# Four DRAM tensors of a hybrid layer kernel in another layout: transposed keys and queries by chunk, neighbourhood values by pair of heads and column block

## The chip, the cores and the metric

The kernel runs on one core of a Trainium2 chip. Five engines work side by side, each through its own instructions in order: TensorE (PE in the profile; PEld is its weight load), VectorE (DVE), ScalarE (ACT), GpSimd (POOL) and SyncE (SP). SP does no arithmetic here; it issues the kernel's DMAs, which run on 16 DMA engines. The metric is the device time of one execution in microseconds, lower is better; a version's time is the median of several runs.

## The reference

One layer over 1024 latent tokens (a grid of 16 rows by 64 columns) and 256 context tokens, width 1024. After a modulated RMS norm and one input projection the columns are split between two groups.

```python
dn_c, s_ctx_f, s_ctx_b = gated_deltanet(pc[..., :DN_IN], ..., s_zero, s_zero)
dn_x, _, _ = gated_deltanet(px[..., :DN_IN], ..., s_ctx_f, s_ctx_b)
qx, kx, vx = na_qkv(px[..., DN_IN:], na_q_norm_w[i], na_k_norm_w[i])
qc, kc, vc = na_qkv(pc[..., DN_IN:], na_q_norm_w[i], na_k_norm_w[i])
na_x = neighborhood_attention(qx, kx, vx, kc, vc, na_rpb[i], rows)
x = x + g1 * (jnp.concatenate([dn_x, na_x], axis=-1) @ w_out[i])
x = x + g2 * swiglu(modulate(rms_norm(x, norm2_w[i]), sh2, sc2), w_ffn_in[i], w_ffn_out[i])
```

Group A (`gated_deltanet`, 4 heads of 128) passes q, k and v through a short convolution and scans them in chunks, forward and backward, context first. In a chunk the state S meets the keys and the queries:

```python
v_new = u_i - jnp.einsum("bhck,bhkv->bhcv", w_i, S)
o_i = (jnp.einsum("bhck,bhkv->bhcv", q_i * jnp.exp(gam_i)[..., None], S)
       + jnp.einsum("bhcm,bhmv->bhcv", qk_i, v_new))
```

Group B (`neighborhood_attention`, 8 heads of 64): each query attends to a window of 8 rows by 16 columns of the grid and to all context keys. The grid's columns are cut into 4 blocks of 16 queries, and a block's keys lie in 32 columns.

## The kernel before

Work runs in stages: modulation and norm; the blocks of the input projection; the scans with the attention beside them; the output projection; the feed-forward part, which takes nearly half of the time. Between the first stages and the scans, intermediate results go through DRAM tensors (names that end in `_d`). The change touches four:

- `kT_d` (128, 4, T): the transposed keys of group A, channel of a head, head, token. `Block.norm` of a "k" block writes one head (L540): 128 pieces of 5 KB.
- `qT_d` (128, 4, L): the same for queries (L544).
- `nv_d` (T, 512): the neighbourhood's values by token. `Wide.tiles` writes it: ten products of 128 tokens, evacuated by ACT into `zt` (L665), stored two at a time (L669), each half of the columns in a `Wide` job of its own.
- `vw_d` (128, 4, 4, 512): partition (four grid rows by 32 columns), column block, row block, the values of all heads. The generator `windows` (L1089) copies it together from `nv_d`, DRAM to DRAM: sixteen copies, one for each column block `cb` and row block `ch`, of 128 pieces of 2 KB (L1093).

The columns of the projection are worked through as `jobs` (L1076): "k" blocks, `Wide(1)`, "nk" blocks, `Wide(0)`, "nk" 3, "nq" blocks, "q" blocks, "v", "z". In the loop at L1109 a job's matmuls are followed by evacuation (`evac`: L491), the square for the norm (L532), `norm` (L549 to L574) and `finish` of the blocks before it. The weights of the next job are fetched by `prefetch`: SP loads 512 KB into `wraw`, of which there is one buffer (L219), ACT casts them into `whi`, of which there are two (L220), GpSimd makes the remainder `wlo` (L222).

Beside the jobs run background generators: `block_inverses` (DVE's eliminations L947 and L949, transposes on PE, results to `x_d` at L969 and L972), then `preps` (fetches L997 to L1003, decays L1015, products L1024). `copies` runs `windows` with two steps behind each k of a job (L1164), from the job after `Wide(0)` on.

Readers of the tensors: a "q" block's `finish` loads its head's keys again as `kTh` (L594). In the scans, `load` (L270) fetches a chunk's `kT` (L280) and `qT` (L289), four heads by 128 tokens: 512 pieces of 512 B each. In the attention, `values` (L329) fetches `vw` for a pair of heads and a column block (L332): again 512 pieces of 512 B. Each of these loads is 256 KB. The loads of `v`, `y`, `kt`, `at` and `kk`, of the same size, have 128 pieces of 2 KB.

The order of instructions on an engine is set by a planner that arranges what the program writes by the times it expects; only where the code asks for it (`pinned`, `held`) is the written order kept. An engine then takes its instructions strictly in that order, and SP its DMAs.

Of the kernel before, what the change touches and what calls it, by code (L numbers as in the profile page):

```python
# [9 lines left out]
F32 = mybir.dt.float32  # L10
# [9 lines left out]
D, L, CT, T = 1024, 1024, 256, 1280  # L20
# [6 lines left out]
NCH = T // 128  # L27
NU = NCH * NH
BLKS = [0, 8, 24, 32]
# [62 lines left out]
def hybrid(ctx, tc, a, dbg):  # L92
    nc = tc.nc
    act, dve, pool, sp = nc.scalar, nc.vector, nc.gpsimd, nc.sync
# [16 lines left out]
    def pools(stack, name, side=None, bufs=1, **kw):  # L111
        if side:
            kw["side"] = side
        return stack.enter_context(tc.tile_pool(name=name, bufs=bufs, reuse_waits="tile", **kw))
# [6 lines left out]
    dram = ctx.enter_context(tc.tile_pool(name="dram", bufs=1, space=DRAM))  # L121
# [37 lines left out]
    v_d = dram.tile([T, 512], F32, name="v_d", tag="v_d")  # L159
    k_d = dram.tile([T, 512], F32, name="k_d", tag="k_d")  # L160
    zT_d = dram.tile([128, 4, L], F32, name="zT_d", tag="zT_d")
    kT_d = dram.tile([128, 4, T], F32, name="kT_d", tag="kT_d")
    qT_d = dram.tile([128, 4, L], F32, name="qT_d", tag="qT_d")
    kk_d = dram.tile([128, NCH, 4, 128], F32, name="kk_d", tag="kk_d")
    qk_d = dram.tile([128, 8, 4, 128], F32, name="qk_d", tag="qk_d")
    nv_d = dram.tile([T, 512], F32, name="nv_d", tag="nv_d")
    nq_d = dram.tile([NAH, 2, ND, L], F16, name="nq_d", tag="nq_d")
    nk_d = dram.tile([2, NAH, ND, T], F16, name="nk_d", tag="nk_d")
    vw_d = dram.tile([128, 4, 4, 512], F32, name="vw_d", tag="vw_d")
    y_d = dram.tile([2, NCH, 128, 4, 128], F32, name="y_d", tag="y_d")  # L170
    at_d = dram.tile([2, 8, 128, 4, 128], F32, name="at_d", tag="at_d")
    x_d = dram.tile([128, 2, 2, NU, 32], F32, name="x_d", tag="x_d")
# [97 lines left out]
    def load(d, c, own=None):  # L270

        def tile(n):
            if own:
                return own.tile([128, 4, 128], F32, name=n, tag=f"{n}{d}")
            return (scan_v if n == "v" else scan_in).tile([128, 4, 128], F32, name=n, tag=n, bufs=3)

        old = chunks.pop(c, None)
        kT, qT, kt, v = old or (tile("kT"), tile("qT") if c >= 2 else None, tile("kt"), tile("v"))
        if not old:
            sp.dma_start(kT, kT_d[:, :, c * 128:(c + 1) * 128])  # L280
            sp.dma_start(fl(v), v_d[c * 128:(c + 1) * 128])
        y = tile("y")
        sp.dma_start(y, y_d[d, c])
        if not old:
            sp.dma_start(fl(kt), k_d[c * 128:(c + 1) * 128])
        at = None
        if c >= 2:
            if not old:
                sp.dma_start(qT, qT_d[:, :, (c - 2) * 128:(c - 1) * 128])  # L289
            at = tile("at")  # L290
            sp.dma_start(at, at_d[d, c - 2])
        if not old and c in TWICE:
            chunks[c] = kT, qT, kt, v
        ready[d, c] = kT, qT, kt, v, y, at
# [5 lines left out]
    def attention(nw):  # L300
# [18 lines left out]
        def biases(hp, half, cb):  # L319

            key = hp, half, CASE[cb]
            if tables[0] != key:
                out = lasting_bt[tables[1] % 2]
                for u, w0 in enumerate(WIN):
                    sp.dma_start(out[u][:, w0:w0 + 384], a["rpb"][2 * hp + u, half, CASE[cb]])
                tables[:] = key, tables[1] + 1
            return lasting_bt[(tables[1] - 1) % 2]

        def values(hp, half, cb):  # L329
            if (hp, cb) not in blocks:  # L330
                vw = nw.tile([128, 4, 128], F32, name="vw", tag="vw", bufs=3)
                sp.dma_start(vw, vw_d[:, cb, :, hp * 128:hp * 128 + 128])  # L332
                blocks[hp, cb] = vw
            return blocks[hp, cb][:, half:half + 3]

# [57 lines left out]

        order = [(hp, half, cb) for hp in range(NAH // 2) for cb, half in TILES]
        heads = {0: [load(0), load(1)]}
        vcs = {0: context(0)}
        bt, vw = biases(*order[0]), values(*order[0])
        yield 1
        old = None
        for n, (hp, half, cb) in enumerate(order):  # L400
            at = n % len(TILES)
            if at in (4, 6) and hp + 1 < NAH // 2:
                heads.setdefault(hp + 1, []).append(load(2 * hp + at // 2))
                if at == 4:
                    vcs[hp + 1] = context(hp + 1)
            cur = pair(heads[hp], bt, vw, vcs[hp], half, cb, na[hp])
            next(cur)
            if old:
                next(old)
            if n + 1 < len(order):  # L410
                bt, vw = biases(*order[n + 1]), values(*order[n + 1])
            yield 1
            if old:
                next(old)
            old = cur
            yield 1
# [5 lines left out]
    with ExitStack() as bs:  # L422
        wp = pools(bs, "wpb", "right", 2)
        shift(bs, "hpad", "right", 64)
        hp = pools(bs, "hp", "right")
# [4 lines left out]
        def bank(name="m"):  # L430

            if len(psum) == 1:
                return psum[0].tile([128, 512], F32, name=name, tag="ps")
            return psum[1].tile([128, 512], F32, name=name, tag=name, bufs=4 if name == "blk" else 2)
# [19 lines left out]
        class Block:  # L454
# [79 lines left out]
            def norm(self):  # L534

                kind, acc, t0, i = self.kind, self.acc, self.t0, self.i
                if kind in "vz":
                    return
                if kind == "k":
                    sp.dma_start(kT_d[:, i], acc)  # L540
                    return
                r = self.r
                if kind == "q":
                    sp.dma_start(qT_d[:, i], acc[:, t0:])  # L544
                    return
                for s0, n in self.segs:
                    p = bank("pr" if kind == "nk" and s0 >= 768 else "m")
                    pe.matmul(p[:, :n], M[C_BD2], r[:, s0:s0 + n], start=True, stop=True)
                    act.activation(r[:, s0:s0 + n], p[:, :n], AF.Ln, bias=b_eps, scale=1.0 / ND)  # L549
                if kind == "nq":  # L550
                    act.activation(r[:, t0:], r[:, t0:], AF.Exp, scale=-0.5, bias=b_naq)
                else:
                    act.activation(r[:, t0:], r[:, t0:], AF.Exp, scale=-0.5)
                isk = kind == "nk"
                u = acc
                dve.scalar_tensor_tensor(u[:, t0:], u[:, t0:], qkw[:, isk:isk + 1], r[:, t0:],
                                         op0=OP.mult, op1=OP.mult)
                hl16 = cp.tile([128, 2, T], F16, name="hl16", tag="kx", bufs=3)
                h16, l16 = hl16[:, 0], hl16[:, 1]
                if isk:  # L560
                    act.copy(h16, u)
                    dve.tensor_tensor(l16, u, h16, OP.subtract)
                else:
                    for hf in range(2):
                        s = slice(t0 + hf * 512, t0 + hf * 512 + 512)
                        uv = u[:, s].rearrange("p (r b c) -> p b r c", r=8, b=4)
                        hv, lv = (x[:, s].rearrange("p (b r c) -> p b r c", b=4, r=8) for x in (h16, l16))
                        act.copy(hv, uv)
                        dve.tensor_tensor(lv, uv, hv, OP.subtract)
                for i, x in enumerate((h16, l16)):  # L570
                    for hb in range(2):
                        hd = 2 * self.i + hb
                        dst = nk_d[i, hd] if isk else nq_d[hd, i]
                        sp.dma_start(dst, x[hb * 64:hb * 64 + 64, t0:])  # L574

            def finish(self):
                kind, acc, i = self.kind, self.acc, self.i
                if kind in "kv":
                    vt = cp.tile([128, NCH, 128], F32, name="vt", tag="kx", bufs=3)
                    for g, m in ((0, 4), (4, 4), (8, 2)):  # L580
                        p = bank()
# [9 lines left out]
                    sp.dma_start(dst[:, i * 128:(i + 1) * 128].rearrange("(c p) d -> p c d", p=128), vt)  # L591
                if kind == "q":
                    kT = cp.tile([128, T], F32, name="kTh", tag="kx", bufs=3)
                    sp.dma_start(kT, kT_d[:, i])  # L594
                    p, r, t0 = bank(), self.r, self.t0
                    for c in range(8):
                        pe.matmul(p[:, c:c + 1], r[:, t0 + c * 128:t0 + (c + 1) * 128], M[C_ONE][:, 0:1],
                                  start=True, stop=True)
                    dve.tensor_copy(SQ[:, :, i], p[:, 0:8])
                    yield  # L600
                else:
                    kT = acc
                if kind in "kq":
                    c0 = 0 if kind == "k" else 2
                    kk = cp.tile([128, NCH, 128], F32, name="kk", tag="kx", bufs=3)
                    for g in range(c0, NCH, 4):
                        m = min(4, NCH - g)
                        p = bank()
# [480 lines left out]
        def windows():  # L1089
            vlat = nv_d[CT:].rearrange("(r c) d -> r c d", c=64)  # L1090
            for cb in range(4):
                for ch in range(4):
                    sp.dma_start(vw_d[:, cb, ch], vlat[4 * ch:4 * ch + 4, BLKS[cb]:BLKS[cb] + 32])  # L1093
                    yield

        copies = Background()
# [12 lines left out]
        for n in range(2, len(jobs) + 2):  # L1109
# [59 lines left out]
            if isinstance(j, Wide) and n == values:  # L1169
                copies.add(windows())  # L1170
# [202 lines left out]
    acc = nrm.tile([128, L], F32, name="acc", tag="acc")  # L1373
# [488 lines left out]
```

## Time and profile before

| | |
|---|---|
| median of three runs | 1512.64 us (1511.35 to 1515.03) |
| the profiled execution | 1511.45 us |
| its span, first to last instruction | 1509.7 us |
| mean granted TensorE clock | 0.99 |
| DMA moved | 267.35 MB in 198851 packets, of which 106960 under 2 KB |

Stages, from the chain in order of time: projection blocks to about 552 us, scans and attention from there to about 770 us, output projection to about 860 us, feed-forward to the end. The page gives, part by part, each engine's busy time, the span in 40 slices, the DMA queues, and the chain of work that ended last. Views of the trace give the same for chosen stretches: a timeline lists instructions in order of time (start, duration, engine and line, operation, out<-in by name, count), the waits name who waited for whom (us in total, times, longest), and the view of a tensor gives the durations of its instructions (least, median, most in ns). "SPq" is SP issuing a DMA: its duration is that of the issue, not of the transfer. In the chain, "DMA a<-b" is the time from the issue to the landing.

### The profile page before, as it was taken

The page shows a single profiled execution, that of the slowest core. Times are in us where ns is not written, and L with a number is a line of the kernel's source. Part 1 is how long each engine was busy: PE and PEld are TensorE (multiplying, and loading weights), DVE is VectorE, ACT ScalarE, POOL GpSimd, SP SyncE. Part 2 cuts the span into 40 slices and gives each one's busy share as a digit, 9 for nine tenths or more (in the row PEclk, how much of TensorE's full clock was granted, in tenths as well). Part 3 has the DMA queues.
Part 4 walks back from the last instruction along what each step waited for, and adds up shares of the span by engine and source line. Part 5 has one row for each costly group of instructions (what it writes and reads, how often), then busy time and mean ns, then how long its engine had stood idle before and what let it go on. Part 6 is the DMA issues. An engine that isn't in the chain of part 4 may idle for free.

```text
span 1509.7 us, 23086 instructions
## 1 busy us (share of the span) xinstructions
PE 1453.5 (96%) x8365; PEld 1205.7 (80%) x8365; DVE 1007.9 (67%) x1908; ACT 704.7 (47%) x1379; POOL 164.6 (11%) x191
## 2 busy tenths in 40 slices
PE   6999998799999999999989999999999999999998
PEld 2789887678877778898777888788888888888887
DVE  4886579445587418789966499655555666698652
ACT  6443362585256536667732374333333334354441
POOL 0153500243134300000000000000000000000000
PEclk9999999999999999999999999999999999999999
DMA  9377133566378799986339216333333325798742
GB/s 366 119 237 234 35 107 121 180 180 194 98 235 249 214 272 289 264 225 184 116 119 313 99 35 208 106 105 105 105 105 105 104 94 173 267 365 281 237 153 84
DMA packets 198851, 267.35 MB, mean 177 GB/s; under 512 B 15232, under 2 KB 106960, under 8 KB 197712
## 3 DMA queue, kind: packets, MB, share of 16 engines
q1 hardware_dynamic: 198016, 265.49, 55.1%
q8 instruction: 66, 1.08, 0.3%
q10 hardware_dynamic: 720, 0.37, 0.1%
q14 instruction: 49, 0.40, 0.1%
HBM read 201.01 MB, written 68.98 MB: 179 GB/s over the span
## 4 chain that ended last, share of the span: by engine, by line
PE 67%; DVE 8%; DMA 5%; ACT 5%; issue 2%; SPq 1%; POOL 0%; ACTq 0%; DVEq 0%; POOLq 0%
PE ps L102 45%; PE blk L102 10%; PE sc L102 5%; PE pr L102 3%; DMA nv_d<-zt 2%; PE sc L106 2%; PE m L102 1%; DMA wad<-wa 1%; DMA wraw<-w_nqk 1%; DVE acc L256 1%; ACT ex L366 1%; DVE x L1616 1%; DVE cacc L520 1%; SPq L1093 1%; DVE ex L368 0%
## 5 line engine op out<-in xcount | busy, mean ns | idle before, releaser
L102 PE MATMUL ps<-hT,uhi 128*128 128x512 f32 x496 | 146.8, 390 | 0.9 <-DVE e L1737 0.8
L102 PE MATMUL ps<-lT,uhi 128*128 128x512 f32 x496 | 146.4, 389 | 0.0
L102 PE MATMUL ps<-hT,ulo 128*128 128x512 f32 x496 | 146.2, 389 | 0.0
L102 PE MATMUL blk<-hh,whi 128*128 128x512 f32 (+1 forms) x456 | 139.3, 397 | 2.1 <-ACT hh L748 1.8
L102 PE MATMUL blk<-hl,whi 128*128 128x512 f32 (+1 forms) x456 | 130.1, 379 | 0.0
L102 PE MATMUL blk<-hh,wlo 128*128 128x512 f32 (+1 forms) x456 | 129.9, 378 | 0.0
L102 PE MATMUL ps<-hB,uhi 128*128 128x512 f32 x436 | 129.1, 390 | 0.0
L102 PE MATMUL ps<-lB,uhi 128*128 128x512 f32 x436 | 128.9, 389 | 0.0
L102 PE MATMUL ps<-hB,ulo 128*128 128x512 f32 x436 | 128.7, 389 | 0.0
L1446 ACT CAST uhi<-ws 128x512 fp32r<-128x512 f32 x91 | 54.7, 623 | 145.4 <-PE ps L102 75.8
L1446 ACT CAST uhi<-wq 128x512 fp32r<-128x512 f32 x101 | 60.4, 621 | 130.8 <-PE ps L102 66.3
L1447 DVE TENSOR_TENSOR ulo<-wq,uhi 128x512 fp32r<-128x512 f32 x101 | 67.1, 686 | 65.6 <-ACT uhi L1446 36.1
L102 PEld LDWEIGHTS ps<-hT,uhi 128*128 128x128 f32 x496 | 92.9, 188 | 20.7 <-ACT uhi L1446 1.2
L102 PEld LDWEIGHTS ps<-lT,uhi 128*128 128x128 f32 x496 | 93.0, 188 | 19.7 <-DVE lT L1600 0.4
L102 PEld LDWEIGHTS ps<-hT,ulo 128*128 128x128 f32 x496 | 93.1, 188 | 19.4
L102 PEld LDWEIGHTS ps<-hB,uhi 128*128 128x128 f32 x436 | 81.8, 188 | 17.4 <-issue 0.5
L102 PEld LDWEIGHTS ps<-lB,uhi 128*128 128x128 f32 x436 | 81.8, 188 | 17.3 <-DVE lB L1600 0.4
L102 PEld LDWEIGHTS ps<-hB,ulo 128*128 128x128 f32 x436 | 81.8, 188 | 17.0
L102 PEld LDWEIGHTS blk<-hh,wlo 128*128 128x128 f32 x456 | 80.9, 191 | 17.9 <-issue 1.7
L102 PEld LDWEIGHTS blk<-hl,whi 128*128 128x128 f32 x456 | 81.6, 192 | 15.5
L102 PEld LDWEIGHTS blk<-hh,whi 128*128 128x128 f32 x456 | 77.3, 192 | 19.4 <-ACT hh L748 3.7
L1447 DVE TENSOR_TENSOR ulo<-ws,uhi 128x512 fp32r<-128x512 f32 x91 | 60.6, 685 | 36.2 <-ACT uhi L1446 28.1
(337 smaller groups left out, 3020.1 us busy)
## 6 DMA issues: line engine op xcount, KB each, us to landing
wq<-w_fo SPq DMA_DIRECT2D x99, 256.0 KB
wq<-w_gu SPq DMA_DIRECT2D x88, 256.0 KB
wad<-wa SPq DMA_DIRECT2D x64, 256.0 KB
t_d<-g SPq DMA_DIRECT2D x22, 512.0 KB
fr<-t_d SPq DMA_DIRECT2D x44, 256.0 KB
bt<-rpb SPq DMA_DIRECT2D x48, 192.0 KB
f_d<-g SPq DMA_DIRECT2D x33, 256.0 KB
fr<-f_d SPq DMA_DIRECT2D x33, 256.0 KB
```

The costliest lines, as they stand in the source:

```text
L102: i = nc.tensor.matmul(*args, **kw)
L106: i = nc.tensor.transpose(*args, **kw)
L256: dve.scalar_tensor_tensor(acc2, x, sc, acc2, op0=OP.mult, op1=OP.add)
L366: act.activation(ex, ex, AF.Exp, bias=m[:, 1:2], accum_out=m[:, 2:3])
L520: dve.scalar_tensor_tensor(acc[:, d0:d1], raw[:, d0 + o:d1 + o], cw[:, blk, tap:tap + 1], acc[:, d0:d1], op0=OP.mult, op1=OP.add)
L1093: sp.dma_start(vw_d[:, cb, ch], vlat[4 * ch:4 * ch + 4, BLKS[cb]:BLKS[cb] + 32])
L1446: act.copy(hi, self.raw[key])
L1447: dve.tensor_tensor(lo, self.raw[key], hi.bitcast(F32), OP.subtract)
L1616: dve.tensor_tensor(B[at][:, k], B[x][:, k], B.get(y, B["B11"])[:, k], OP.subtract)
```

## The change

The four tensors are declared, written and read in another order of dimensions. `kT_d` and `qT_d` get the chunk ahead of the head; `vw_d` gets the pair of heads ahead of the column block, and its last dimension is 128, one pair. A load in the scans or the attention then takes 128 pieces of 2 KB. The stores of `kT_d` and `qT_d` and the reload `kTh` go by chunk, in pieces of 512 B. `windows` copies one grid row at a time, 32 columns by four pairs of heads: 64 copies of 128 pieces of 512 B, four ahead of each `yield` where there was one. No arithmetic changes.

```diff
-    kT_d = dram.tile([128, 4, T], F32, name="kT_d", tag="kT_d")
-    qT_d = dram.tile([128, 4, L], F32, name="qT_d", tag="qT_d")
+    kT_d = dram.tile([128, NCH, 4, 128], F32, name="kT_d", tag="kT_d")
+    qT_d = dram.tile([128, 8, 4, 128], F32, name="qT_d", tag="qT_d")
...
-    vw_d = dram.tile([128, 4, 4, 512], F32, name="vw_d", tag="vw_d")
+    vw_d = dram.tile([128, 4, 4, 4, 128], F32, name="vw_d", tag="vw_d")
...
-            sp.dma_start(kT, kT_d[:, :, c * 128:(c + 1) * 128])
+            sp.dma_start(kT, kT_d[:, c])
...
-                sp.dma_start(qT, qT_d[:, :, (c - 2) * 128:(c - 1) * 128])
+                sp.dma_start(qT, qT_d[:, c - 2])
...
-                sp.dma_start(vw, vw_d[:, cb, :, hp * 128:hp * 128 + 128])
+                sp.dma_start(vw, vw_d[:, hp, cb])
...
-                    sp.dma_start(kT_d[:, i], acc)
+                    sp.dma_start(kT_d[:, :, i], acc.rearrange("p (c t) -> p c t", t=128))
...
-                    sp.dma_start(qT_d[:, i], acc[:, t0:])
+                    sp.dma_start(qT_d[:, :, i], acc[:, t0:].rearrange("p (c t) -> p c t", t=128))
...
-                    sp.dma_start(kT, kT_d[:, i])
+                    sp.dma_start(kT.rearrange("p (c t) -> p c t", t=128), kT_d[:, :, i])
...
             vlat = nv_d[CT:].rearrange("(r c) d -> r c d", c=64)
             for cb in range(4):
                 for ch in range(4):
-                    sp.dma_start(vw_d[:, cb, ch], vlat[4 * ch:4 * ch + 4, BLKS[cb]:BLKS[cb] + 32])
+                    for r in range(4):
+                        sp.dma_start(vw_d[r * 32:r * 32 + 32, :, cb, ch], vlat[4 * ch + r, BLKS[cb]:BLKS[cb] + 32]
+                                     .rearrange("c (h d) -> c h d", h=4))
                     yield
```

## The prediction

> **What bounds the kernel now.** I read the page first: the engines' shares, then the chain that ended last.
>
> ```profile
> span 1509.7 us, 23086 instructions
> PE 1453.5 (96%) x8365; PEld 1205.7 (80%) x8365; DVE 1007.9 (67%) x1908; ACT 704.7 (47%) x1379; POOL 164.6 (11%) x191
> PE 67%; DVE 8%; DMA 5%; ACT 5%; issue 2%; SPq 1%; POOL 0%; ACTq 0%; DVEq 0%; POOLq 0%
> ```
>
> TensorE is busy for 1453.5 of 1509.7 us, so at most 56 us of its idle time can be won by anything that moves data faster; DMA has 5% of the chain. The question is where that 5% lies and whether the tensors of this change are in it. The chain in order of time, asked for the stretch from 250 to 303 us, names them:
>
> ```profile
> 250.33 11.45 DMA nv_d<-zt
> ...
> 264.59 12.16 DMA wraw<-w_nqk
> 276.75 0.02 issue
> ...
> 293.40 3.59 DMA x_d<-WK
> 296.99 0.02 issue
> 297.01 3.12 DMA kk<-kk_d
> ```
>
> Two transfers take 11.45 and 12.16 us here, where others land in 3 to 4. What lies in front of them is seen in the timeline of SP's queue (start, time, line, tensors, count):
>
> ```profile
> 219.71 1.07 SPq L669 DMA_DIRECT2D nv_d<-zt  x2
> 223.28 3.15 SPq L1093 DMA_DIRECT2D vw_d<-nv_d  x4
> 228.79 0.37 SPq L669 DMA_DIRECT2D nv_d<-zt  x1
> ...
> 240.11 10.12 SPq L1093 DMA_DIRECT2D vw_d<-nv_d  x6
> 250.33 2.36 SPq L669 DMA_DIRECT2D nv_d<-zt  x1
> 252.73 11.76 SPq L1093 DMA_DIRECT2D vw_d<-nv_d  x5
> 264.59 2.38 SPq L219 DMA_DIRECT2D wraw<-w_nqk  x1
> ```
>
> These are the sixteen copies of `windows` (L1093), DRAM to DRAM, 256 KB each. The table by stretches of time (us; then PE, PEld, DVE, ACT, POOL; granted clock, DMA share, GB/s) shows how they run:
>
> ```profile
> 256.00:258.00 2.00, 2.00 (x11) 1.65 (x10) 1.93 (x3) 0.00 (x0) 0.00 (x0) 1.00 0.26 102
> 258.00:260.00 2.00, 1.90 (x9) 1.24 (x7) 1.93 (x3) 0.00 (x0) 0.00 (x0) 1.00 0.26 101
> 260.00:262.00 2.00, 0.00 (x0) 0.00 (x0) 1.90 (x3) 0.00 (x0) 0.00 (x0) 1.00 0.27 100
> ```
>
> The copies are waiting in line, and yet only 0.26 of the 16 DMA engines is busy and about 101 GB/s move: four engines carry them. 16 x 256 KB are 4.19 MB; at 0.101 MB/us that is 41.5 us, most of the time from the first copy's issue at 223.28 to the moment the weight load behind them lands, 276.75.
>
> The rule behind this is in the Trainium skill, DMA: Bandwidth & Descriptors, Queues, rings and completion order (as it tells why a DMA increments its semaphore by 16): a DMA runs on the largest number of engines up to 16 that divides the outermost dimension of both sides. The source of a copy before has four grid rows outermost, so the rule gives 4, and the trace agrees (0.26 of 16). By the same rule a copy of after, one row of 32 columns against 32 partitions, gets 16.
>
> **Who feels it.** The waits between engines, 250 to 310 us:
>
> ```profile
> ACT whi L220 <- DMA wraw<-w_nqk: 21.4, 1, 21.4
> PE pr L102 <- DVE kk L1016: 7.0, 1, 7.0
> PE m L106 <- DVE N L952: 5.4, 1, 5.4
> ```
>
> PE itself is idle twice. The 5.4 us end with DVE's block inverses, which no transfer of this change feeds. The 7.0 us, up to 302.25 us, end with the first decay of `preps`, and the chain leads from there back over x_d, DVE and ACT to the late weight load: ACT could not cast it before 276.85, and its later work in order (the evacuation L491, the norm L549 to L553) stood behind.
>
> **The change part by part.** The time goes against the profiled execution: 1511.45 us with 1.75 us outside its span of 1509.7; the median of the three runs, 1512.64, is 1.19 above it.
>
> *The copies of `windows`.* 64 issues of 64 KB stand where 16 of 256 KB stood, four behind each yield. Bytes are the same, pieces are 512 B instead of 2 KB, 8192 instead of 2048. Over 16 engines the transfer is no longer the limit: in the scan, a mix of 512 B and larger pieces goes at 281 GB/s (row below), and 4.19 MB at that rate are 15 us. SP's issue time takes its place.
>
> ```profile
> L1093 SPq DMA_DIRECT2D vw_d<-nv_d x16: 589/703/2514, 223.3 to 263.7; - x16
> L669 SPq DMA_DIRECT2D nv_d<-zt x10: 360/597/2357, 115.4 to 250.3; - x10
> L624 SPq DMA_DIRECT2D kk_d<-kk x4: 562/570/577, 96.7 to 153.6; - x4
> L998 SPq DMA_DIRECT2D kk<-kk_d x20: 319/366/882, 297.0 to 498.2; - x20
> ```
>
> (Nanoseconds, least, median, most.) An issue of the new copy is not in the trace. From below the nearest is 319 ns, the least of a load of 128 pieces; from above 703 ns, the median of the old copy, whose long ones of 2.4 to 2.5 us, like those of nv_d and wraw, are issues into engines that are full. I take 570 ns, the store in 512 B pieces at the same stride. 64 x 0.57 = 36.5 us, and the bounds give 20 and 45.
>
> I walk SP's order as it was, with four copies for each one. The first 16 go from 223.3 to 232.4. The third nv_d store is out at 232.8 and lands at 235.6 (the chain shows 2.78 us for the store at 219.71, before the copies). With four nk_d stores of 0.5 us, 4 copies and the fourth store, SP stands at 239.3; that store lands at 242. 24 copies end at 253; the last store lands at 256 rather than 261.8; 20 copies end at about 265. So the weight load is issued at 265, where it was 264.6, but it meets free engines: 4 us (3.59 for x_d is the nearest) instead of 12.16. It lands at 269. Now something else is late: the buffer of the cast. `whi` has two buffers, and the one that comes free is read by the block whose last matmuls are these (timeline of PE):
>
> ```profile
> 273.91 0.62 PE L102 MATMUL blk<-hh,wlo 128*128 128x512 f32 x2
> 274.38 1.45 PE L102 MATMUL m<-cr,cst 128*128 128x256 f32 x4
> ```
>
> So the cast moves from 276.85 to about 274.1: **2.75 us**. ACT, DVE and the fetches behind it move with it, and PE's wait of 7.0 us becomes 4.2. With issues of 319 ns the floor at 274.1 is the same; with 703 ns the 64 copies end at 273, the load lands at 277.5, and the cast is 0.7 us later than it was.
>
> The trace shows that SP's order is planned and not the program's (nv_d's last store is written ahead of all copies and issued after eleven of them). 48 more instructions can move what stands around them, by a few us either way; this I keep in the range.
>
> *Loads of the scan.* 16 kT, 14 qT and 16 vw loads have 128 pieces of 2 KB for 512 of 512 B.
>
> ```profile
> L280 SPq DMA_DIRECT2D kT<-kT_d x16: 518/554/789, 525.7 to 723.9; - x16
> L289 SPq DMA_DIRECT2D qT<-qT_d x14: 523/524/758, 558.7 to 729.7; - x14
> 540.00:550.00 10.00, 10.00 (x46) 8.29 (x45) 0.00 (x0) 1.09 (x2) 0.00 (x0) 1.00 1.00 364
> 560.00:640.00 80.00, 77.73 (x759) 69.19 (x760) 62.23 (x204) 55.09 (x151) 0.00 (x0) 1.00 1.04 281
> DVE vn L1223 <- DMA at<-at_d: 0.7, 1, 0.7
> ```
>
> The DMA engines are full from 560 to 640 us, and the mix with 512 B pieces moves 281 GB/s against 364 in a stretch of larger ones. 46 loads are 12.06 MB: 42.9 us at the one rate, 33.1 at the other, 9.8 us less of DMA time, an upper bound. SP saves about 0.2 us on 30 of them (0.55 to 0.33). But PE has 2.27 us idle in all those 80 us, and the waits from 520 to 770 us name a load's landing once, 0.7 us. Loads come a chunk ahead. I count 0; the bound is 2.3 us of gain from 560 to 640. A loss could only come from loads that arrive earlier and crowd others; buffers still set when they start, so I count none.
>
> *Stores and the reload.* Eight stores (kT_d, qT_d) and four loads of kTh go in 512 B pieces, 1280 or 1024 where there were 128.
>
> ```profile
> L540 SPq DMA_DIRECT2D kT_d<-cacc x4: 326/382/476, 80.3 to 130.5; - x4
> ```
>
> Issue grows from 0.38 to 0.57 us, 12 x 0.2 = 2.4 us of SP in stages where PE has other blocks; kk_d is stored in this form already. Transfer: 640 KB take 2.3 us at 281 GB/s and 1.8 at 364, half a microsecond each. No engine's wait names kT_d, and `kTh` is waited for by none in its own view. I count 0; if the cover were gone, it would be 12 x 0.7 = 8 us.
>
> Sum: 1511.45 - 2.75 = 1508.7 for the profiled execution, and with the 1.19 us **1509.9 us** against the median.
>
> **The rivals.**
>
> *SP becomes the bound (slower).* Beyond 0.70 us an issue, the copies push the weight load past the old landing. At 1 us an issue the same walk (waits for stores included) ends at about 292, and the load lands at 296, 20 us later than before. PE needs its cast when the block before it is through, whose evacuation is this row:
>
> ```profile
> 289.87 1.09 ACT L491 ACTIVATE cacc<-blk 128x512 f32<-128x512 f32 x2 [0.67 <-DVE hl L562]
> ```
>
> PE would wait from there to about 298: 8 us, 1521. Half of that, 1517 to 1518, is the likelier form. For it: the old copy's median, 0.70. Against it: the medians of all other rows here are under 0.6. The Trainium skill, DMA: Bandwidth & Descriptors, Rules for kernel authors, is on this side: coalesce many small transfers, those under 64 KB are mostly overhead; the new copies are just 64 KB. No run here shows such a copy.
>
> *The stall has another end (no change).* After 277 the path passes ACT, DVE's L970 (3.6 us) and SP's order of x_d, e, xc and kk. If one of these is planned differently, the 2.75 us are lost at the next: 1512.6.
>
> *More comes back.* PE's idle time in the scan (2.3 us) and more of the 4.2 us left at 302 go too: 1512.64 - 2.75 - 4.5 = 1505.4.
>
> *The order settles otherwise.* Planned order shifts beyond 310 us, by some 5 us to either side: 1505 or 1517.
>
> **How the numbers follow.** Chances: forecast 0.38, SP the bound 0.18, no change 0.16, more comes back 0.16, another order 0.12 (half each side). 0.3%, about what a measurement of this kernel can tell from no change, is 4.5 us: under 1508.1 is faster, over 1517.2 slower. Faster holds "more", half of "another order" and a quarter of the forecast: 0.32. Slower holds SP the bound and a little of another order: 0.22. The rest, 0.46, is within. The range leaves out the far half of "SP the bound" and the deepest gains: 1502 to 1518.5.
>
> **What would show it.** Right: between 223 and 270 us the DMA share in stretches with copies alone is well over 0.26 when they move, or the copies are gaps of issue; no issue of 2.4 us; the weight load lands in 4 us; the cast follows PE's matmul and not the load; PE's wait at 300 us shrinks to about 4; issues of kT and qT fall to 0.33 us and the scan's length stays. Wrong: new copies of over 0.7 us, a cast that still waits for wraw, a longer wait at 300 us, or a scan that is shorter by more than 2.3 us.

## The result and the profile after

| | median | runs |
|---|---|---|
| before | 1511.35 us (1508.03 to 1515.03) | 5 |
| after | 1533.7 us (1530.92 to 1537.53) | 5 |

The ratio is 1.0143, 95% interval 1.0125 to 1.0161: slower by some 22 us, on the other side of the forecast and outside its range. The profiled execution of after took 1530.92 us. Its page, the same three lines as were shown of before:

```profile
span 1529.1 us, 23134 instructions
...
PE 1454.2 (95%) x8365; PEld 1205.3 (79%) x8365; DVE 1005.4 (66%) x1908; ACT 705.3 (46%) x1379; POOL 158.2 (10%) x191
...
PE 66%; DVE 11%; ACT 5%; DMA 4%; issue 2%; POOL 1%; SPq 0%; ACTq 0%; DVEq 0%; POOLq 0%
```

TensorE does the same 1454 us of work in a span that is 19.4 us longer, so all of the loss is idle time of PE. DMA's share of the chain fell from 5% to 4% and DVE's rose from 8% to 11%. So the added time is not spent on transfers; something else is waited for.

**Where it lies.** Steps that both kernels have in common mark the stages in the chain in order of time: the last of the four stores of `zT_d`, with which the projection blocks end; the load of the output projection's weights; and a product early in the feed-forward part. Before, then after:

```profile
552.87 2.99 DMA zT_d<-zt
777.77 4.31 DMA wraw<-w_out
945.52 0.47 PE ps L102
```

```profile
569.21 2.90 DMA zT_d<-zt
794.28 4.62 DMA wraw<-w_out
964.98 0.47 PE ps L102
```

At the last `zT_d` store after is 16.3 us behind. Over the scans the gap grows by 0.2 us (224.9 us before, 225.1 after), from there to the third step by 2.95 us. So the stage with all the loads that were made better moved by nothing, and most of the loss is made ahead of it. The sums of the table by stretches, 250 to 360 us (PE, PEld, DVE, ACT, POOL busy), find nearly all of it in those 110 us. Before and after:

```profile
sum 110.00, PE 97.57 PEld 76.30 DVE 63.34 ACT 65.51 POOL 41.34; mean PE 8.87 PEld 6.94 DVE 5.76 ACT 5.96 POOL 3.76
```

```profile
sum 110.00, PE 81.73 PEld 61.69 DVE 50.53 ACT 60.57 POOL 29.41; mean PE 7.43 PEld 5.61 DVE 4.59 ACT 5.51 POOL 2.67
```

PE lost 15.8 us there. The waits of after, 250 to 350 us, and the timeline of SP's queue show how:

```profile
PE pr L102 <- DVE kk L1016: 17.4, 1, 17.4
DVE cacc L556 <- ACT cr L551: 8.4, 1, 8.4
```

```profile
240.31 0.54 SPq L669 DMA_DIRECT2D nv_d<-zt  x1
240.89 31.49 SPq L1094 DMA_DIRECT2D vw_d<-nv_d  x49
272.72 0.34 SPq L969 DMA_DIRECT2D x_d<-WK  x1
...
283.86 2.61 SPq L574 DMA_DIRECT2D nk_d<-hl  x4
296.45 0.33 SPq L969 DMA_DIRECT2D x_d<-ut  x1
301.38 0.33 SPq L972 DMA_DIRECT2D x_d<-WK  x1
301.80 0.38 SPq L997 DMA_DIRECT2D e<-g_d  x1
302.23 0.90 SPq L999 DMA_DIRECT2D xc<-x_d  x1
...
306.28 0.61 SPq L219 DMA_DIRECT2D wraw<-w_nqk  x1
```

The wait of 7.0 us at 302 did not shrink to 4; it is 17.4 us and ends at 310. Two things are late. The weight load, which stood directly behind the copies at 264.59, is issued at 306.28, and this is no matter of SP's time: between 272 and 301 us SP stands idle for most of it. The load has another **place in SP's order**, behind the stores of `x_d` and the first fetches of the decays. And the second half of `x_d` is stored at 301.38 where it was 293.40, because DVE's second transposition (L967) has another place too. Timeline of DVE, before and then after:

```profile
285.40 1.55 DVE L556 SCALAR_TENSOR_TENSOR cacc<-cacc,qkw,cr 128x1280 f32<-128x1280 f32 x1 [8.62 <-ACT cr L553]
286.87 1.50 DVE L967 STREAM_TRANSPOSE ut<-WK 128x1280 f32<-128x1280 f32 x1
```

```profile
293.72 1.28 DVE L556 SCALAR_TENSOR_TENSOR cacc<-cacc,qkw,cr 128x1024 f32<-128x1024 f32 x1 [8.36 <-ACT cr L551]
294.92 1.51 DVE L967 STREAM_TRANSPOSE ut<-WK 128x1280 f32<-128x1280 f32 x1
299.26 0.69 DVE L569 TENSOR_TENSOR hl<-cacc,hl 128x512 f16<-128x512 f32 x1 [2.84 <-ACT hl L568]
299.87 1.48 DVE L970 TENSOR_TENSOR WK<-WK,NB 128x1280 f32<-128x1280 f32 x1
```

The transposition needs nothing from the norm of the next block (L556), yet stands behind it in DVE's order, and that norm waits 8.36 us for ACT. So neither the decays nor the next block's weights are there when PE has run out of work. The planner has arranged this stretch anew, on every engine; the load and the transposition are the two late places that bear on PE here.

### The profile page after: what moved, and what is told of

Same layout as the page of the kernel before. It is cut to its first block, busy times and chain, and to the rows that moved or that the text cites. A ratio compares the mean times of both kernels' runs of the same rounds, so it can differ in the third digit from the quotient of the medians.

```text
span 1529.1 us, 23134 instructions
## 1 busy us (share of the span) xinstructions
PE 1454.2 (95%) x8365; PEld 1205.3 (79%) x8365; DVE 1005.4 (66%) x1908; ACT 705.3 (46%) x1379; POOL 158.2 (10%) x191
## 4 chain that ended last, share of the span: by engine, by line
PE 66%; DVE 11%; ACT 5%; DMA 4%; issue 2%; POOL 1%; SPq 0%; ACTq 0%; DVEq 0%; POOLq 0%
PE ps L102 45%; PE blk L102 11%; PE sc L102 5%; PE pr L102 3%; PE sc L106 2%; DVE N L949 2%; DVE tt L947 2%; DMA wad<-wa 1%; PE m L102 1%; PE m L106 1%; DVE acc L256 1%; DMA xc<-x_d 1%; ACT ex L366 1%; DVE x L1618 1%; DVE ex L368 0%
## 5 line engine op out<-in xcount | busy, mean ns | idle before, releaser
L102 PEld LDWEIGHTS ps<-hT,ulo 128*128 128x128 f32 x496 | 93.1, 188 | 19.4
L102 PEld LDWEIGHTS ps<-hB,uhi 128*128 128x128 f32 x436 | 81.8, 188 | 17.4 <-issue 0.5
```

What stands on the lines that cost most here:

```text
L102: i = nc.tensor.matmul(*args, **kw)
```

## The experiments

Four theories were to be told apart. A: the loss is in the order that the planner writes (the load's place, or that and `x_d`). B: it is SP's time for 48 more issues. C: it is the pieces of 512 B, or the keys' and queries' scattered stores. D: the copies at 16 engines crowd other transfers. The kernel before was run again with each group of variants, on the same chip, and had medians of 1510.67 to 1513.65 us; each ratio is taken against its own group. The first decay product on PE (`pr<-fx,kk`) and the last `zT_d` store, from one profiled execution each, say where each variant stands. e1 and e7, which have the order of before on every engine, show how much such a mark moves by itself: 0.7 and 1.1 us.

| | first decay on PE | last `zT_d` store | median | ratio, 95% interval |
|---|---|---|---|---|
| before | 302.25 | 552.87 | 1511.35 | |
| after | 310.08 | 569.21 | 1533.7 | 1.0143 [1.0125, 1.0161] |
| e1 keys and queries alone | 303.37 | 553.59 | 1515.01 | 1.0007 [0.9992, 1.0023] |
| e2 values alone | 309.81 | 570.22 | 1530.91 | 1.0108 [1.0078, 1.0139] |
| e3 sixteen copies, sixteen engines | 308.86 | 567.14 | 1533.94 | 1.0125 [1.0095, 1.0156] |
| e4 changed, load ahead | 312.42 | 565.80 | 1529.62 | 1.0114 [1.0077, 1.0151] |
| e5 changed, copies later | 297.43 | 550.72 | 1513.25 | 1.0002 [0.9986, 1.0017] |
| e6 as e3, copies later | 297.22 | 558.32 | 1520.04 | 1.0033 [1.0004, 1.0062] |
| e7 before, copies later | 301.60 | 551.79 | 1511.93 | 0.9992 [0.9976, 1.0007] |
| e8 before, load behind | 295.64 | 560.24 | 1525.51 | 1.0105 [1.0073, 1.0136] |

**One half of the change at a time (e1, e2).** e1 has the new layout of `kT_d` and `qT_d` with their stores and loads, and `vw_d` with its sixteen copies as before. e2 has the reverse: the new `vw_d` with its 64 copies, keys and queries as before.

> Only the layout of the keys and queries is changed; the copies of the neighbourhood's values are as before, and the planned order of every engine is the one of before. Theory A (planned order: what costs 22 us is that the weight load of the block nq 2 is planned behind the fetches of preps, so that PE's wait before the first decay is 17 us instead of 7): within 2 us of before, PE's wait stays at 7 us. Theory B (SP's issue time of the 48 added copies): the same, as none is added. Theory C (pieces of 512 B are slow): slower by several us, as the twelve stores and reloads in small pieces are all here. If loads in pieces of 2 KB help the scans, up to 10 us faster; the forecast counted 0 for them.

> Only the neighbourhood's values are changed, with 64 copies of 64 KB; the planned order is the one of the changed kernel on every engine. Theories A and B: all of the loss, 20 to 24 us above before, weight load issued at about 306 us, PE's wait 17 us. Theory C with the keys as its seat: near before.

Keys and queries are worth nothing that can be measured, and e1's order of instructions is that of before on every engine. The values carry the loss, with the order of after on every engine: 18.5 us by the medians, a little less than was expected, and the interval overlaps that of after.

**Sixteen fast copies (e3).** The kernel before with its own layouts and its own sixteen copies in 2 KB pieces; only the dimensions of a copy are turned, so that 32 columns are outermost on both sides.

```diff
-                    sp.dma_start(vw_d[:, cb, ch], vlat[4 * ch:4 * ch + 4, BLKS[cb]:BLKS[cb] + 32])
+                    sp.dma_start(vw_d[:, cb, ch].rearrange("(r c) d -> c r d", c=32),
+                                 vlat[4 * ch:4 * ch + 4, BLKS[cb]:BLKS[cb] + 32].rearrange("r c d -> c r d"))
```

> Layouts of before and sixteen copies in pieces of 2 KB as before, but each copy with the 32 columns outermost on both sides. It adds no issue and no small piece. The plan, however, sets the weight load of nq 2 behind x_d and the first fetches, as in the changed kernel. Theory A: slower than before by 14 to 22 us, PE's wait before the first decay about 17 us. Theory B: at or below before, since SP has no more to issue (0 to -3 us). Theory C: at or below before. On either theory, if the outermost dimension sets the number of DMA engines, the DMA share beside the copies is no longer flat at 0.26 and the last of them is issued well before 265 us, with no issue of 2.4 us.

The copies are fast, and SP is free early. The table by stretches of e3 (columns as before; granted clock, DMA share and GB/s stand last), and its SP queue:

```profile
243.00:247.00 4.00, 4.00 (x23) 3.38 (x22) 3.86 (x5) 0.00 (x0) 0.00 (x0) 1.00 0.91 272
247.00:251.00 4.00, 4.00 (x21) 3.08 (x19) 3.90 (x4) 1.42 (x3) 0.29 (x1) 1.00 1.01 363
```

```profile
236.93 10.72 SPq L1093 DMA_DIRECT2D vw_d<-nv_d  x12
...
271.16 0.34 SPq L969 DMA_DIRECT2D x_d<-WK  x1
...
304.78 0.62 SPq L219 DMA_DIRECT2D wraw<-w_nqk  x1
```

```profile
308.86 2.02 PE L102 MATMUL pr<-fx,kk 128*128 128x96 f32 x8 [17.71 <-DVE kk L1016]
```

No issue has been added, no piece made smaller, the last copy is issued at 247 us, and SP then stands idle for 23 us: yet the loss is the same, with the load at 304.78 and PE's wait at 17.71 us. That refutes B and C. It speaks against D too: from 251 us on the DMA engines are all but idle (share 0.04 from 251 to 255 us, 0.00 from 255 to 259), long before anything in this queue is late. What e3 does share with after is the order: apart from the copies themselves, the instructions of all five engines stand in the same sequence in both. The one thing that e3 changes is the shape of the copies, which here is enough for another order.

**Only the load taken back (e4).** After, with the weights of that block fetched one job earlier in the program:

```diff
-            if n + 1 < len(jobs):
+            if n + 1 < len(jobs) and n != 11:
                 jobs[n + 1].prefetch()
+            if n == 10:
+                jobs[n + 2].prefetch()
```

> The changed kernel, with one edit: the weight load of nq 2 is written one job earlier, which sets it on SP right behind the 64 copies and ahead of x_d and the fetches. The 64 copies stand all ahead of it. Theory A: PE's wait before the first decay falls to 2 to 7 us and the time comes back to within 5 us of before (1506 to 1517), the load being issued at about 272 us and landing in 4. Theory B: little changes, since the load still stands behind 64 issues: 1525 or more.

A miss for the narrow form of A. The load is issued early and PE's long wait is gone, but `x_d` is as late as in after and the idle time is spread out instead:

```profile
270.70 0.61 SPq L219 DMA_DIRECT2D wraw<-w_nqk  x1
...
301.64 0.33 SPq L972 DMA_DIRECT2D x_d<-WK  x1
```

```profile
312.42 2.02 PE L102 MATMUL pr<-fx,kk 128*128 128x96 f32 x8 [4.18 <-DVE kk L1016]
```

By the `zT_d` store this gives back 3.4 us of 16.3; the interval of the ratio overlaps that of after. Part of the reason is that only the load came back: its cast (L220) stands behind the next block's norm in ACT's order and begins at 291.78, where before has 276.85. Once the rest of the order has moved, the load's place on SP by itself is a small part.

**The order taken back (e5, e6, with e7 as control).** After, unchanged in its 64 copies and all layouts, except that the program enters `windows` among the background work at a later job; the planner then sets the load, its cast and the transposition early again. e6 does this to e3, and e7 to the kernel before.

```diff
-            if isinstance(j, Wide) and n == values:
+            if n == 12:
                 copies.add(windows())
```

(In e6 and e7 the number is 11. Before and after enter the copies behind job 8, so this is four and three jobs later, not the two that the expectations name; the planner still sets the first copies at about 222 us in all three.)

> The changed kernel with its 64 copies written two jobs later in the program (from the job nq 1 on). All 64 are still made, in the same pieces. The plan then spreads them between other transfers: the weight load of nq 2 stands behind 33 of them, and DVE's second transposition for x_d stands again where it stood before the change. Theory A in its wider form (the loss is the planned order as a whole: the late weight load and the late second half of x_d together): 1505 to 1517, first decay product on PE by 304 us. Theory B (the copies' issues themselves): 1525 or more.

> The sixteen copies with the columns outermost (layouts of before), written two jobs later. Theory A: as the run before it, 1505 to 1515, and if the forecast's 2.75 us from copies on sixteen engines are there once the order is in place, rather 1506 to 1511. If the copies' spread over more engines is itself harmful: still above 1520.

> A control: the kernel before with its own sixteen copies on four engines written two jobs later. The plan keeps the place of the weight load behind all copies and changes only details after 300 us. Theory A: within 5 us of before. It shows how much such a step moves by itself.

In e5 the loss is gone, with every copy, issue and piece of the change still there. SP's queue of e5:

```profile
240.01 11.37 SPq L1094 DMA_DIRECT2D vw_d<-nv_d  x18
254.48 0.60 SPq L219 DMA_DIRECT2D wraw<-w_nqk  x1
255.13 7.92 SPq L1094 DMA_DIRECT2D vw_d<-nv_d  x12
...
287.34 0.33 SPq L972 DMA_DIRECT2D x_d<-WK  x1
```

```profile
297.43 2.02 PE L102 MATMUL pr<-fx,kk 128*128 128x96 f32 x8 [4.45 <-DVE kk L1016]
```

The load is out at 254.48 behind 33 of the copies (the 18 shown and 15 ahead of them), `x_d` at 287.34, and PE's first decay at 297.43, 4.8 us ahead of before. From the load on this is the forecast's path: the cast begins at 273.00, after 18.74 us of waiting that PE's matmul ends and not the load, and PE's wait is 4.45 us, where the forecast had 4.2. It comes to nothing all the same: at the `zT_d` store 2.15 us of it are left, and the control e7, with the order of before, has 1.1 us there by itself; the medians are equal.

e5 also thins the copies out (the last is issued at 331 us, in after at 272). That this, and not the order, brings the time back is not ruled out by e5 alone; e3, whose copies are all but over by 251 us and which has the whole loss, speaks against it.

e6 missed its expectation by 5 us. It starts well (first decay at 297.22), but the planner has put the load of the next block behind the stores of `nq_d`, at 320.57 instead of 309.86, and PE stands for 3.06 us:

```profile
318.12 2.41 SPq L574 DMA_DIRECT2D nq_d<-hl  x4
320.57 0.61 SPq L219 DMA_DIRECT2D wraw<-w_conv  x1
```

```profile
335.88 0.74 PE L102 MATMUL blk<-hh,whi 128*128 128x512 f32 x2 [3.06 <-ACT whi L220]
```

Its median of 1520.04 just reaches what was expected if the spread over more engines were itself harmful. e6 alone does not decide that, since its order is neither that of before nor that of e5; e5, whose copies go over sixteen engines too and which loses nothing, does.

**The mirror (e8).** The kernel before, with no copy touched, and only this one load held in the written order behind the first fetches:

```diff
-                sp.dma_start(r, src)
+                i = sp.dma_start(r, src); hold[0] and tc.keep_in_program_order(i)
...
-                jobs[n + 1].prefetch()
+                hold[0] = n == 11; jobs[n + 1].prefetch(); hold[0] = False
```

> The kernel before with its own layouts and its own 16 copies, in which only the weight load of the block nq 2 is held in SP's order behind the first fetches of the decay products, as in the changed kernel; the planner then moves what stands around it, but VectorE's second turn of x_d stays in its old place in the order, ahead of the first decay product. Theory A1 (the place of this one load in SP's order carries the whole loss): the load is issued 40 us later, at 300 to 306, PE waits for 14 us or more in one piece, and the time is 1527 to 1535. Theory A2 (the load carries only the 3 to 5 us that the load put ahead gave back, and the late second half of x_d the rest, so that here the decay products fill PE's wait): the second WK store is issued at 288 to 294 as before, the first decay product is at 297 to 303, and the time is 1514 to 1520. Theory B/C (the copies themselves, by SP's issue or by traffic, make the loss): no copy is changed, so 1509 to 1514.

1525.51 us, between the two forms of A; the load is issued at 292.24, 28 us later than before and not the 40 of A1. SP's queue, and PE's first decay:

```profile
285.37 0.32 SPq L972 DMA_DIRECT2D x_d<-WK  x1
...
292.24 0.61 SPq L219 DMA_DIRECT2D wraw<-w_nqk  x1
```

```profile
295.64 2.02 PE L102 MATMUL pr<-fx,kk 128*128 128x96 f32 x8 [5.21 <-DVE kk L1016]
```

The second half of `x_d` is early, as A2 said, so the decays come before the weights instead of after them; PE still has too little to do between 285 and 310 us, and the last `zT_d` store is 7.4 us late in the profiled execution, which was the fastest of its four (1519.05 to 1528.96). So a late load, with what the planner moves around it and without any change to a copy, costs 11 to 21 us by the interval of the ratio. The price of one instruction's place depends on where the others stand: taken back alone (e4) it returned 3.4 us, moved alone it cost 7.4 by the same mark.

## Why the prediction was wrong

**What held.** The limit was read rightly: the copies before ran on four DMA engines, and with another outermost dimension they run on sixteen (share 0.26 before, 0.91 to 1.01 in e3). This is the rule of the Trainium skill, DMA: Bandwidth & Descriptors, Why a DMA increments its semaphore by 16 and not by 1, and these rows bear it out for transfers between DRAM tensors. The estimate of 570 ns for an issue of the new copies was near the median of 596, and the condition of the rival "SP becomes the bound", more than 0.70 us an issue, was not met. The view of the tensors of after (count; least, median, most in ns):

```profile
L1094 SPq DMA_DIRECT2D vw_d<-nv_d x64: 469/596/1791, 222.4 to 271.8; - x64
L280 SPq DMA_DIRECT2D kT<-kT_d x16: 319/327/777, 542.0 to 740.1; - x16
L289 SPq DMA_DIRECT2D qT<-qT_d x14: 319/323/602, 575.0 to 745.9; - x14
L540 SPq DMA_DIRECT2D kT_d<-cacc x4: 525/537/578, 81.8 to 132.0; - x4
```

The loads of kT and qT fell to 0.33 us an issue, the store of kT_d rose to 0.54 (forecast 0.57), and both were rightly costed at nothing: e1 is 1.0007, and the scans kept their 225 us. The prediction said that the waits from 520 to 770 us name a load's landing once; the view has two more, both of ACT: 8.7 us put down to the load of `v`, ahead of the scans, and 3.1 us for the store of `zT_d` at their start. PE's own waits in the scans name no landing, before or after, so the count of 0 stands. The rate argument was looser than it looked: with the larger pieces that stage moves 282 GB/s, no more than the 281 of before, while PE is busy for 97% of it in both.

```profile
576.00:656.00 80.00, 77.49 (x758) 69.11 (x758) 62.01 (x204) 55.26 (x151) 0.00 (x0) 1.00 0.95 282
```

Only the DMA engines' share fell, from 1.04 to 0.95, for the same bytes in the same 80 us, and PE's busy time there is 77.49 us, against 77.73.

**The step that failed** is "I walk SP's order as it was, with four copies for each one." From it followed a load issued at 265, landing at 269, and a cast at 274.1: -2.75 us. Instead the planner wrote another order: the load was issued at 306.28 and its cast began at 312.73, the second half of `x_d` was stored at 301.38, and PE's wait was 17.4 us where the forecast had 4.2. The trace of before had shown that the order is planned; the prediction said so and then kept the old order for everything but the copies. e3, e5 and e8 show the premise to be wrong in both directions: another order with no added instruction, and the old time with all 48 of them.

**The rival that came nearest** was "the order settles otherwise", with a chance of 0.12 and 5 us to either side. Its mechanism was right and its size was not: the new order, with the load and one transposition late in it, cost 16.3 us by the last `zT_d` store. The size could have been bounded from the trace of before. The chain ran through this load, and a load of the weights that comes after the first decays leaves PE nothing but the decays, which themselves wait; the working counted that price, 8 us, only for slow issues.

**And the term itself.** The walk was too quick as well. In after the last copy's issue ended at 272.4 us, not at 265: 49 of them in a row took 0.64 us each. Behind them a load that lands in 4.2 us, as those of `w_conv` do in after, would let the cast begin at about 276.6, an estimate from these two times: hardly ahead of the 276.85 of before. Nor does an earlier cast yet make a shorter kernel. e5 has it, and an earlier first decay, and a ratio of 1.0002 [0.9986, 1.0017], which leaves at most some 2 us. The nearest rival is "the stall has another end", but in e5 the gain is lost behind the first decay, later than that rival says; where it goes was not traced.

**What stays open.** Why the planner chose this order for faster copies was not traced in its working; only that the copies' shape is enough (e3). How the 16.3 us divide between the load, its cast and the transposition is open too: e4 and e8 each move more than one of them. The 2.95 us that after lost behind the scans are not explained: e2, with the same order on every engine, takes 168.5 us there (797.40 to 965.85 in the chain), where before takes 167.8 and after 170.7.

## What to carry to other kernels

Where a planner sets the order, a change of a DMA's shape or number is also a change of the order around it: ask first which instructions on the chain have a free choice of place, and price their worst place, not only the transfer that is edited. Compare the order of the two kernels before reading durations, and if a faster transfer makes a kernel slower, try the same transfers entered at another time in the program. Look first whether the bounding engine waits for a landing: here the scans were full of DMA traffic, but PE waited for none there, and wider pieces paid nothing.

## What was not expected of the hardware

With pieces of 512 B the 64 copies on sixteen engines are limited by SP's issue, not by the engines: 49 issues in a row take 31.49 us, and 64 KB each 0.64 us are 102 GB/s. While they run in after, the share is 0.36 and 103 GB/s move, hardly more than the 101 GB/s of four engines before, where e3's sixteen larger copies reach 363 GB/s.

```profile
243.00:251.00 8.00, 8.00 (x42) 6.78 (x41) 7.76 (x8) 0.10 (x1) 0.00 (x0) 1.00 0.36 103
```

The granted clock falls with PE's idle time. In the last 10 us of after's 17.4 us of waiting it is 0.50, and it stays there at first when PE works again. In the 10 us from the first decay on it averages 0.67 in after, and 0.74 in before, whose wait was 7.0 us. The rows here go by fixed stretches of 10 us; that of before still holds 2.25 us of its wait. After, then before:

```profile
300.00:310.00 10.00, 0.00 (x0) 0.00 (x0) 5.11 (x6) 4.35 (x13) 2.44 (x7) 0.50 0.72 218
310.00:320.00 10.00, 9.26 (x53) 7.53 (x53) 2.15 (x5) 7.43 (x23) 7.67 (x15) 0.66 0.84 271
```

```profile
300.00:310.00 10.00, 7.75 (x45) 6.12 (x45) 3.82 (x6) 7.20 (x23) 7.12 (x16) 0.66 0.72 216
```
